# Seven-product pairs in the down projection, with one of their weight sums made ahead through HBM

## The chip, the cores and the metric

One Trainium2 chip, one of its NeuronCores. The metric is device time in microseconds (us) of one execution of the whole program; the kernel before takes 1456.75 us (median of 3 runs, 1456.52 to 1457.44). Everything is computed to fp32 quality: each factor x is split into a high part (`fp32r`, made by a copy on ScalarE) and a low part x - high (made by a subtraction on VectorE), and a product is the sum of high·high, high·low and low·high. One product of weights and activations is therefore three matmuls.

## The reference

One encoder layer over 256 tokens with a model width of 2048. What matters here is its second half:

```python
hf = rms_norm(x, ffn_norm)
g  = dwconv_centred(hf @ w_ffn_gate, conv_w, conv_b)       # 2048 -> 5632
x  = x + (gelu(g) * (hf @ w_ffn_up)) @ w_ffn_down          # 5632 -> 2048
gate_p = sigmoid(rms_norm(x, ple_norm) @ w_ple_gate)       # 2048 -> 2048
x  = x + gate_p * (p @ w_ple_proj)
out = rms_norm(x, final_norm)
```

Before it come one input projection, two attention branches, their projections, gates and an output projection.

## The kernel before, in words

The weights lie in HBM as a list of pieces of 128 x 2048 fp32 (1 MB), in the order of use. SyncE (SP) loads them one after another into three rotating buffers `raw` (L245). A piece is cut into units. For each unit ScalarE copies it to a high part `uh` or `vh` (L265) and VectorE subtracts to get the low part `ul` or `vl` (L266). Units made straight from the weights go through a ring of six, the `u` ring; units made from sums of weights go through a ring of two, the `v` ring. `drop` frees a unit when the last matmul on it is written, and `pump` then lets the next be made. TensorE (PE) consumes them.

The stages after the attention, in order, with the names used below:

- **E0 and E1**: the MLP halves. Each makes 22 chunks of 128 gate columns and 22 of up columns. One chunk of either is a *job*: 16 matmuls of 512 columns (L309) and 16 of 256 (L316), on one piece of weights. When a job is done `mlp` gathers it from PSUM (L447, L451); for every second gate chunk it does the convolution and gelu (L977 to L988), for every second up chunk the product (L997, L998), and it then splits the result into high and low (L1006, L1007, or L458, L459).
- **F00, F01 and F10, F11**: the down projection of the first and second half, each in two column ranges of 1024 of the model. One piece holds two chunks of rows (a *pair*) times two column blocks of 512, so it is a 2x2 by 2x2 block product. Kind `s` does it in eight products of 3 matmuls of 512 columns, 24 matmuls. Kind `S` does it in seven products, 21 matmuls, by sums of weights and sums of activations (a Strassen scheme). The sums of weights are made on VectorE from the loaded piece (L258 to L260), those of the activations by `sums_of` (L838 to L844).
- **pp0, pp1 and G0, G2, G3**: the per-layer embedding, its projection and the last gate. G0 also alternates seven and eight products; G2 and G3 do not.

`DOWN = "SsSsSsSsSss"` gives the kinds of the eleven pairs of each F stage: five of eleven by seven products. `ALT`, used by G0 among others, is `"SsSsSsSs"`. At the end of each F stage `row_sums` combines the seven products' accumulators on VectorE (L814 to L817) and adds them to the residual rows (L927, L929), while the last piece is still being multiplied.

Each engine runs its own instructions strictly in order, and that order is fixed when the program is built: a scheduler takes the program's order and its own estimate of costs, and may move instructions past one another unless they are marked with `keep`, which holds them in program order. `run_due` runs work that was put with `at` at a certain step of a stage: `at((stage, k), f)` runs `f` when the stage's loop reaches step k.

Of the kernel before, what the change touches and what calls it, by code (L numbers as in the profile page):

```python
# [16 lines left out]
P = 128  # L17
# [78 lines left out]
DOWN = "SsSsSsSsSss"  # L96
# [14 lines left out]
def _pieces():  # L111
# [8 lines left out]
    def quads(stage, n0, n1, pattern, k0=0):  # L120
        stages[stage] = range(len(pieces), len(pieces) + len(pattern))
        for i, c in enumerate(pattern):
            a, b = k0 + 2 * i, k0 + 2 * i + 1
            pieces.append((c, [(n0, a), (n1, a), (n1, b), (n0, b)]))
# [16 lines left out]
    for half in range(2):  # L141
        names = {"g": "w_ffn_gate", "u": "w_ffn_up"}
        jobs = [(names[kind], f) for kind, f in _ffn(half)]
        joint = 0 if half else JOINT
        e = [(name, k, f) for k in range(KC) for name, f in jobs[:joint]]
        e += [(name, k, f) for name, f in jobs[joint:] for k in range(KC)]
        blocks("E%d" % half, e)
        for s in range(2):
            quads("F%d%d" % (half, s), ("w_ffn_down", 2 * s * WIDE), ("w_ffn_down", (2 * s + 1) * WIDE),
                  DOWN, half * FHALF)  # L150
# [4 lines left out]
    quads("G0", ("w_ple_gate", 0), ("w_ple_gate", WIDE), ALT)  # L155
# [9 lines left out]
def _unit_list():  # L165

    units, of = [], []
    for p, (kind, _) in enumerate(_PIECES):
        if p == 0:
            cuts = [("n", a * P, b * P) for a, b in ((0, 1), (1, 4), (4, 7), (7, 11), (11, PIECE))]  # L170
        elif kind == "S":
            cuts = [("n", 0, WIDE), ("n", 2 * WIDE, 4 * WIDE), ("T13", 0, 2 * WIDE), ("T24", 2 * WIDE, 4 * WIDE)]
        else:
            cuts = [("n", 0, 2 * WIDE), ("n", 2 * WIDE, 4 * WIDE)]
        of.append(list(range(len(units), len(units) + len(cuts))))
        units += [(p, *cut) for cut in cuts]
    return units, of
# [11 lines left out]
def _encoder(ctx: ExitStack, tc, xt, pt, xrow, cols, gainrow, table, onehot, mask, ident_in, wts, out):  # L189
# [22 lines left out]

    flat = big.tile([P, KC + KC * T], F32, name="x", tag="R1")
# [28 lines left out]
    def load(r, a=0, b=PIECE):  # L242
        if a == 0:
            raws[r] = wpool.tile([P, PIECE * P], F32, name="raw", bufs=3)
        nc.sync.dma_start(raws[r][:, a * P:b * P], wts[r][:, a * P:b * P])  # L245
        state["raw"] = r + 1

    def produce():
# [7 lines left out]
        if kind == "T13":  # L256
            q = [raw[:, i * WIDE:(i + 1) * WIDE] for i in range(4)]
            nc.vector.tensor_tensor(raw[:, :2 * WIDE], raw[:, WIDE:3 * WIDE], raw[:, :2 * WIDE], op=ALU.subtract)  # L258
            nc.vector.tensor_tensor(q[2], q[2], q[0], op=ALU.subtract)
            nc.vector.tensor_tensor(q[3], q[3], q[2], op=ALU.subtract)  # L260
        src = raw[:, a:b]
# [4 lines left out]
        nc.vector.tensor_tensor(lo, src, hi.bitcast(F32), op=ALU.subtract)  # L266
        made[u] = (hi, lo)
# [105 lines left out]
    def quad_stage(stage, moving, combos=None, tags=("M2", "M3", "M4", "P22")):  # L373
# [24 lines left out]
        for i, p in enumerate(pieces):  # L398
            kind = _PIECES[p][0]
            us = _UNITS_OF[p]  # L400
            a, b = moving(2 * i), moving(2 * i + 1)
# [8 lines left out]
            else:  # L410
                s = combos(i)
                sums = [(s[:, 0, e], s[:, 1, e]) for e in range(4)]
                for g, (name, stationary, u, c, gone) in enumerate((
                        ("M1", part(a, 0), 0, 0, 0), ("M7", sums[2], 2, 1, None), ("M5", sums[0], 2, 0, 2),
                        ("M6", sums[1], 3, 0, None), ("M4", part(b, 1), 3, 1, 3),
                        ("M2", part(b, 0), 1, 1, None), ("M3", sums[3], 1, 0, 1))):
# [79 lines left out]
    def rms(i, total, key, columns=HALVES):  # L496
# [5 lines left out]
        at(i[0], ask)  # L502

# [103 lines left out]

    def view(a, offset, *dims):
        return bass.AP(tensor=a.tensor, offset=a.offset + offset, ap=[a.ap[0], *([step, n] for step, n in dims)])
# [223 lines left out]
    def sums_of(u, tag):  # L833
# [8 lines left out]
        s = tok.tile([P, 2, 4, P], FR, name="S", tag="S%d" % tag)  # L842
# [4 lines left out]
    combos = {}  # L847
# [113 lines left out]
    def activation_row(k):  # L961
        k %= FHALF
        return held["act"][1][k - 16] if 16 <= k < 20 else held["act"][k // 20 * 2][:, k - k // 20 * 20, :]
# [4 lines left out]
    def mlp(kind, n, acc):  # L968
# [21 lines left out]
        else:  # L990
# [8 lines left out]
            m = n % FHALF - 1  # L999
            if 16 <= m < 20:  # L1000
                for i in range(2):
                    halves(activation_row(m + i), u[:, i])
            else:
                i = m // 20 * 2
                d = held["act"][i][:, m - 10 * i:m - 10 * i + 2]
                nc.scalar.activation(d[:, :, :T], u, AF.Copy)  # L1006
                nc.vector.tensor_tensor(d[:, :, T:], u, d[:, :, :T].bitcast(F32), op=ALU.subtract)  # L1007
            pair = m // 2
            if DOWN[pair] == "S":
                combos["act", pair] = sums_of(u, pair // 2)  # L1010
# [13 lines left out]

    for half in range(2):
        held["act"] = [big.tile([P, 16, 2 * T], FR, name="act", tag="R1"),
                       [big.tile([P, 2 * T], FR, name="act1", tag="yb%d" % i) for i in range(4)],
                       held["tok"].tile([P, 2, 2 * T], FR, name="act2")]
# [159 lines left out]
```

## Time and profile before

| | |
|---|---|
| median of 3 runs | 1456.75 us (1456.52 to 1457.44) |
| the profiled execution's own time | 1457.09 us |
| its span, from the first to the last instruction | 1455.3 us, granted TensorE clock 0.998 |
| PE / VectorE / ScalarE busy | 1444.2 / 1196.8 / 838.7 us |
| HBM read, written | 279.49 MB, 2.14 MB |
| E0, F0 (F00 and F01), E1, F1 (F10 and F11) | 627 to 874, 874 to 987, 987 to 1232, 1232 to 1347 us of the span |
| pp0 and pp1, G0 to G3 | 1347 to 1360, 1360 to 1445 us |

The page counts a matmul as busy from its start to its modelled end, and consecutive matmuls overlap. So how fast PE really goes is read from the distance between the starts of two matmuls in the timeline, and a stall is a distance above the usual one. The same holds for VectorE: a 1024-wide operation is listed with 1.22 us, and the next one starts 1.14 us after it.

### The profile page before, as it was taken

To read this page: it belongs to the slowest core of one execution; us is meant where nothing else is said; L and a number is where in the kernel's file an instruction comes from. 1 tells how busy PE (TensorE), PEld (TensorE's weight loads), DVE (VectorE), ACT (ScalarE), POOL (GpSimd) and SP (SyncE) were. 2 spreads that over 40 slices of the span, in tenths; PEclk is the share of its full clock that TensorE was granted. 3 is DMA by queue.
4 is the path that set the end of the run, shared out by engine and by line. 5 is a ranking of instruction groups with operands and counts; after the bars stand their busy time and mean duration, and the time that the engine had idled before them with its cause. 6 is when DMAs were issued, how large, how long until landed. Compare 5 with 4: busy or idle time off the path is not lost.

```text
span 1455.3 us, 19303 instructions
## 1 busy us (share of the span) xinstructions
PE 1444.2 (99%) x7476; PEld 1234.3 (85%) x7476; DVE 1196.8 (82%) x1626; ACT 838.7 (58%) x1132; POOL 4.8 (0%) x9
## 2 busy tenths in 40 slices
PE   9999999999999999999999999999999999999997
PEld 8888888888888888888888888888888888888785
DVE  7677664679998989988787789987877778999994
ACT  7455544456555656666565565455655656565763
POOL 0000000000000000000000000000000000000000
PEclk9999999999999999999999999999999999999999
DMA  9653445535546456465555545465555554546462
GB/s 336 250 205 145 160 162 178 170 141 203 197 186 236 184 209 231 174 233 201 177 194 184 198 147 225 175 253 187 198 178 199 176 201 173 190 193 235 170 234 85
DMA packets 46455, 282.87 MB, mean 194 GB/s; under 512 B 4948, under 2 KB 9940, under 8 KB 14108
## 3 DMA queue, kind: packets, MB, share of 16 engines
q1 hardware_dynamic: 45644, 280.46, 52.8%
q8 instruction: 58, 0.95, 0.3%
q10 hardware_dynamic: 720, 1.19, 0.2%
q14 instruction: 33, 0.27, 0.1%
HBM read 279.49 MB, written 2.14 MB: 194 GB/s over the span
## 4 chain that ended last, share of the span: by engine, by line
PE 97%; DVE 1%; ACT 1%; issue 0%; DMA 0%; POOL 0%; POOLq 0%; DVEq 0%; SPq 0%; ACTq 0%
PE bank L309 29%; PE bank L316 15%; PE bank L366 14%; PE bank L367 14%; PE bank L368 14%; PE bank L355 2%; PE bank L357 2%; PE bank L293 2%; PE bank L356 2%; PE bank L294 1%; PE bank L861 1%; PE bank L678 0%; PE bank L626 0%; PE bank L625 0%; PE bank L624 0%
## 5 line engine op out<-in xcount | busy, mean ns | idle before, releaser
L265 ACT ACTIVATE uh<-raw 128x1024 fp32r<-128x1024 f32 (+2 forms) x519 | 523.1, 1015 | 394.0 <-PE bank L309 163.8
L266 DVE TENSOR_TENSOR ul<-raw,uh 128x1024 fp32r<-128x1024 f32 (+2 forms) x519 | 594.9, 1166 | 162.6 <-issue 81.0
L309 PE MATMUL bank<-hf,uh 128*128 128x512 f32 x1408 | 336.3, 391 | 0.0
L309 PEld LDWEIGHTS bank<-hf,uh 128*128 128x128 f32 x1408 | 258.9, 188 | 50.1
L316 PEld LDWEIGHTS bank<-hf,ul 128*128 128x128 f32 x1408 | 180.4, 191 | 6.7
L316 PE MATMUL bank<-hf,ul 128*128 128x256 f32 x1408 | 182.8, 283 | 0.0
L265 ACT ACTIVATE vh<-raw 128x1024 fp32r<-128x1024 f32 x92 | 97.0, 1056 | 42.4 <-DVE raw L258 22.9
L266 DVE TENSOR_TENSOR vl<-raw,vh 128x1024 fp32r<-128x1024 f32 x92 | 111.8, 1218 | 0.3
L309 PE MATMUL bank<-hs,uh 128*128 128x512 f32 x432 | 103.6, 392 | 0.0
L447 ACT ACTIVATE t<-bank 128x256 f32<-128x256 f32 x122 | 46.5, 383 | 97.4 <-PE bank L316 86.5
L309 PEld LDWEIGHTS bank<-hs,uh 128*128 128x128 f32 x432 | 79.5, 188 | 15.6
L366 PE MATMUL bank<-uh,act 128*128 128x512 f32 x232 | 90.4, 390 | 0.0
L367 PE MATMUL bank<-ul,act 128*128 128x512 f32 x232 | 90.4, 390 | 0.0
L368 PE MATMUL bank<-uh,act 128*128 128x512 f32 x232 | 90.2, 390 | 0.0
L366 PE MATMUL bank<-uh,hs 128*128 128x512 f32 x172 | 67.3, 391 | 0.0
L368 PE MATMUL bank<-uh,hs 128*128 128x512 f32 x172 | 67.2, 391 | 0.0
L367 PE MATMUL bank<-ul,hs 128*128 128x512 f32 x172 | 67.0, 389 | 0.0
L316 PE MATMUL bank<-hs,ul 128*128 128x256 f32 x432 | 56.6, 284 | 0.0
L258 DVE TENSOR_TENSOR raw<-raw 128x1024 f32<-128x1024 f32 x46 | 56.1, 1220 | 0.5
L316 PEld LDWEIGHTS bank<-hs,ul 128*128 128x128 f32 x432 | 54.5, 191 | 1.0
L367 PE MATMUL bank<-vl,S 128*128 128x512 f32 x138 | 54.0, 392 | 0.1
L366 PE MATMUL bank<-vh,S 128*128 128x512 f32 x138 | 54.1, 398 | 0.0
(242 smaller groups left out, 2229.4 us busy)
## 6 DMA issues: line engine op xcount, KB each, us to landing
raw<-in_wts SPq DMA_DIRECT2D x251, 1024.0 KB, 4.8
raw<-in_wts SPq DMA_DIRECT2D x12, 512.0 KB, 6.7
xr<-in_xrow SPq DMA_DIRECT2D x4, 512.0 KB, 8.2
x<-in_xt SPq DMA_DIRECT2D x13, 128.0 KB, 5.6
hb<-hold SPq DMA_DIRECT2D x3, 514.0 KB, 7.0
hb<-hold SPq DMA_DIRECT2D x2, 768.0 KB, 6.5
last<-in_gainrow SPq DMA_DIRECT2D x1, 1024.0 KB, 8.3
out<-xr SPq DMA_DIRECT2D x4, 256.0 KB, 2.6
```

Source lines behind the costliest of these rows:

```text
L258: nc.vector.tensor_tensor(raw[:, :2 * WIDE], raw[:, WIDE:3 * WIDE], raw[:, :2 * WIDE], op=ALU.subtract)
L265: nc.scalar.activation(hi, src, AF.Copy)
L266: nc.vector.tensor_tensor(lo, src, hi.bitcast(F32), op=ALU.subtract)
L293: nc.tensor.matmul(acc, hi[:, w], m, start=first, stop=False, skip_group_check=True)
L309: nc.tensor.matmul(acc, weights(u)[0][:, o * P:(o + 1) * P], m, start=first, stop=False, skip_group_check=True)
L316: nc.tensor.matmul(acc[:, T:], weights(u)[1][:, o * P:(o + 1) * P], m[:, :T], start=False, stop=last, skip_group_check=True)
L355: nc.tensor.matmul(acc[:, :n * P], xh, hi, start=(k == 0), stop=False)
L356: nc.tensor.matmul(acc[:, :n * P], xh, lo, start=False, stop=False)
L366: nc.tensor.matmul(acc, sh, wh, start=first, stop=False)
L367: nc.tensor.matmul(acc, sh, wl, start=False, stop=False)
L368: nc.tensor.matmul(acc, sl, wh, start=False, stop=last)
L447: keep(nc.scalar.activation(t, acc[:, T:], AF.Copy, scale=scale))
```

## The change

A third kind of piece, `Z`, takes the place of `S` in the F stages and in G0. It is a seven-product piece as well, 21 matmuls, with other sums: one sum of three of the four weight blocks is no longer made when the piece is used. It is made ahead, in the MLP halves: the three blocks are loaded once more (half the columns at a time, 128 x 3 x 256), VectorE makes the sum in two operations of 256 columns (L271, L272 of the new kernel), and ScalarE's queue stores it to a tile `ahead` in HBM (L275). When the piece is used, SP loads three of its blocks from the weights (L254) and the fourth place from `ahead` (L255). VectorE then makes the rest in one operation of 512 columns and one of 1024 (L282, L283), where `S` took one of 1024 and two of 512.

The first half's pattern becomes `ZZsZsZsZsZs`, six of eleven; the second half's keeps five of eleven. F00 and F01 each have one more seven-product piece, and each begins with two of them in a row. There are 12 `Z` pieces in F00 and F01, 10 in F10 and F11 and 4 in G0, so 24 half sums are made in E0 and 28 in E1. A half sum is asked for at step 9 of a job, added at step 8 of the next job, and stored at the beginning of the one after that, each held in program order. The activations of a `Z` pair are kept as the three blocks that the products use (`ends`) and the four sums (`S`), in other places than before (`places`, not shown).

```diff
-DOWN = "SsSsSsSsSss"
+DOWN = ("ZZsZsZsZsZs", "ZsZsZsZsZss")
+LASTS = 30
+ASK, ADD, STORE = 9, 8, None
...
+        elif kind == "Z":
+            cuts = [("n", WIDE, 2 * WIDE), ("n", 2 * WIDE, 4 * WIDE), ("T21", 0, 2 * WIDE), ("T03", 2 * WIDE, 4 * WIDE)]
...
+        if _PIECES[r][0] == "Z":
+            nc.sync.dma_start(raws[r][:, WIDE:], wts[r][:, WIDE:])
+            nc.sync.dma_start(raws[r][:, :WIDE], ahead.pop(r))
+        else:
+            nc.sync.dma_start(raws[r][:, a * P:b * P], wts[r][:, a * P:b * P])
...
+    def sum_ahead(p, h, tag):
+        cols = slice(h * T, (h + 1) * T)
+        if h == 0:
+            ahead[p] = dram.tile([P, WIDE], F32, name="ahead%d" % p)
+        q = held["tok"].tile([P, 3, T], F32, name="ahead", tag=tag) if isinstance(tag, str) else tag
+        keep(nc.sync.dma_start(q, wts[p][:, :3 * WIDE].rearrange("p (q c) -> p q c", c=WIDE)[:, :, cols]))
+        def add():
+            keep(nc.vector.tensor_tensor(q[:, 0], q[:, 2], q[:, 0], op=ALU.subtract))
+            keep(nc.vector.tensor_tensor(q[:, 0], q[:, 0], q[:, 1], op=ALU.add))
+        def store():
+            keep(nc.scalar.dma_start(ahead[p][:, cols], q[:, 0]))
+        return add, store
+    def sums_of_weights(raw):
+        q = [raw[:, i * WIDE:(i + 1) * WIDE] for i in range(4)]
+        nc.vector.tensor_tensor(q[1], q[0], q[1], op=ALU.subtract)
+        nc.vector.tensor_tensor(raw[:, 2 * WIDE:], raw[:, 2 * WIDE:], view(q[0], 0, (0, 2), (1, WIDE)), op=ALU.subtract)
...
+        behind = _PIECES[p][0] == "Z" == _PIECES[p - 1][0]
+        if kind == "T21" and not behind:
+            sums_of_weights(raw)
...
+        if behind and u == _UNITS_OF[p][1]:
+            sums_of_weights(raw)
...
+                else:
+                    todo = (("M1", m1, 0, 0, 0), ("M7", sums[2], 2, 1, None), ("M6", sums[1], 2, 0, 2),
+                            ("M5", sums[0], 3, 0, None), ("M4", m4, 3, 1, 3),
+                            ("M2", m2, 1, 1, None), ("M3", sums[3], 1, 0, 1))
...
+    def finish_ahead(stage):
+        for e in list(line):
+            e[0] += 1
+            if e[0] == 1:
+                at((stage, ADD), e[1])
...
+            elif e[0] == 2:
+                e[2]()
+                line.remove(e)
...
-        for kind, n in jobs[joint:]:
+        todo = [(p, h) for p in sevens(half) for h in range(2)]
+        for i, (kind, n) in enumerate(jobs[joint:]):
+            if i > 1 and todo and (i % 2 == 0 or i < LASTS):
+                held["job"] = todo.pop(0), ("act2", "S4")[i % 2]
+                one_ahead(stage)
+            finish_ahead(stage)
             mlp(kind, n, product(stage, lambda k: hf[:, k, :], KC, "e"))
+        assert not todo
+        drain_ahead()
```

How the built program differs is shown at two places of VectorE's order. The first is the middle of E0. Before, a job of the up kind has its gather (L451), the product (L997, L998) and two low parts (L266) there:

```order
L986 SCALAR_TENSOR_TENSOR gw<-gw 128x512
L451 TENSOR_TENSOR pair<-bank,t 128x256
L997 SCALAR_TENSOR_TENSOR pair<-pair,rms 128x512
L988 SCALAR_TENSOR_TENSOR gw<-gw 128x512
L998 TENSOR_TENSOR pair<-pair,gw 128x512
L266 TENSOR_TENSOR ul<-raw,uh 128x1024
```

With the change (lines of the new kernel: L500 is the gather, L306 the low part, L1111 the low part of activations, L271 and L272 the sum ahead) such a stretch of E0 is:

```order
L306 TENSOR_TENSOR ul<-raw,uh 128x1024
L1111 TENSOR_TENSOR act<-pair,act 128x2x256
L500 TENSOR_TENSOR gw<-bank,t 128x256
L271 TENSOR_TENSOR ahead<-ahead 128x256
L272 TENSOR_TENSOR ahead<-ahead 128x256
L306 TENSOR_TENSOR ul<-raw,uh 128x1024 x2
L500 TENSOR_TENSOR pair<-bank,t 128x256
L271 TENSOR_TENSOR ahead<-ahead 128x256
```

The two additions stand ahead of the next job's low parts, and whatever they wait for, the low parts wait for too. The second place is the end of F00 and the beginning of F01, where `row_sums` meets the first pieces of F01. Before:

```order
L266 TENSOR_TENSOR ul<-raw,uh 128x1024 x2
L266 TENSOR_TENSOR vl<-raw,vh 128x1024
L927 TENSOR_TENSOR xr<-xr,bank 128x512 x3
L929 TENSOR_TENSOR xr<-xr,c 128x1024
L266 TENSOR_TENSOR ul<-raw,uh 128x512
L266 TENSOR_TENSOR ul<-raw,uh 128x1024
L927 TENSOR_TENSOR xr<-xr,bank 128x512
```

With the change (L891 to L894, L1005 and L1007 are the row sums, L282 and L283 the sums of weights):

```order
L306 TENSOR_TENSOR vl<-raw,vh 128x1024
L282 TENSOR_TENSOR raw<-raw 128x512
L306 TENSOR_TENSOR vl<-raw,vh 128x1024
L306 TENSOR_TENSOR ul<-raw,uh 128x1024
L891 TENSOR_TENSOR c<-bank,c 128x512
L283 TENSOR_TENSOR raw<-raw 128x1024
L892 TENSOR_TENSOR c<-bank,c 128x512
L1005 TENSOR_TENSOR xr<-xr,bank 128x512
L893 TENSOR_TENSOR c<-bank,c 128x512
L894 TENSOR_TENSOR c<-bank,c 128x512
L1005 TENSOR_TENSOR xr<-xr,bank 128x512 x2
L1007 TENSOR_TENSOR xr<-xr,c 128x1024
```

After these come, in order, a fourth L1005, a `vl`, the other L1007 and a second `vl`: the low parts of the sums for the second seven-product piece of F01 stand behind the row sums of F00.

More of the change, by code (lines that the diff above doesn't have):

```diff
@@ L400, in quad_stage @@
             us = _UNITS_OF[p]
-            a, b = moving(2 * i), moving(2 * i + 1)
+            if (stage, i) not in ends:
+                a, b = moving(2 * i), moving(2 * i + 1)
             if kind == "s":
@@ L502, in rms, with one_ahead, ask, drain_ahead @@
         at(i[0], ask)
+    line = []
+    def one_ahead(stage):
+        job, where = held["job"]
+        def ask():
+            line.append([0, *sum_ahead(*job, where)])
+        at((stage, ASK), ask)
+    def finish_ahead(stage):
[3 more added lines that the diff above has]
+                at((stage, ADD), e[1])
+                if STORE is not None:
+                    at((stage, STORE), e[2])
+                    line.remove(e)
+            elif e[0] == 2:
+                e[2]()
+                line.remove(e)
+    def drain_ahead():
+        for e in line:
+            if e[0] == 0:
+                e[1]()
+            e[2]()
+        del line[:]
     due, rt, rc, held = {}, {}, {}, {}
```

94 lines of the change are left out of this document (65 added, 29 removed).

## The prediction

> **What bounds the kernel now.** First the page: busy times and the shares of the chain of waits that ended last.
>
> ```profile
> span 1455.3 us, 19303 instructions
> PE 1444.2 (99%) x7476; PEld 1234.3 (85%) x7476; DVE 1196.8 (82%) x1626; ACT 838.7 (58%) x1132; POOL 4.8 (0%) x9
> PE 97%; DVE 1%; ACT 1%; issue 0%; DMA 0%; POOL 0%; POOLq 0%; DVEq 0%; SPq 0%; ACTq 0%
> ```
>
> PE is 97% of the chain. A busy PE need not be at its pace, so I looked for its pace in the timeline, in F00:
>
> ```profile
> 885.36 0.39 PE L366 MATMUL bank<-vh,S 128*128 128x512 f32 x1
> 885.58 0.39 PE L367 MATMUL bank<-vl,S 128*128 128x512 f32 x1
> 885.81 0.39 PE L368 MATMUL bank<-vh,S 128*128 128x512 f32 x1
> ```
>
> A matmul is listed with 0.39 us, but the next starts 0.227 us after it. The windows by stage (PE, PEld, DVE, ACT, POOL busy) say that this is the pace of whole stages:
>
> ```profile
> 627.00:875.00 248.00, 248.00 (x1431) 219.20 (x1430) 195.84 (x289) 149.56 (x210) 0.71 (x1) 1.00 0.53 189
> 875.00:987.00 112.00, 112.00 (x495) 92.58 (x494) 102.79 (x111) 59.30 (x64) 0.00 (x0) 1.00 0.56 211
> 987.00:1232.00 245.00, 245.00 (x1409) 216.50 (x1408) 188.88 (x273) 144.59 (x196) 0.00 (x0) 1.00 0.52 186
> 1232.00:1347.00 115.00, 115.00 (x515) 94.87 (x514) 110.26 (x132) 66.38 (x79) 0.00 (x0) 1.00 0.57 211
> ```
>
> In F0 (second row) 495 matmuls take 112 us, 0.2263 us each: there is no stall to speak of. VectorE, however, is busy 102.8 of these 112 us (92%), and 110.3 of 115 in F1. So PE sets the end, and VectorE is the engine that could take its place. How near it is shows in the timeline after the row sums of F00, VectorE first and then PE:
>
> ```profile
> 941.82 1.22 DVE L266 TENSOR_TENSOR vl<-raw,vh 128x1024 fp32r<-128x1024 f32 x1
> ...
> 943.16 0.39 PE L366 MATMUL bank<-vh,S 128*128 128x512 f32 x1
> 943.38 0.39 PE L367 MATMUL bank<-vl,S 128*128 128x512 f32 x1
> ```
>
> The low part is ready at 941.82 + 1.22 = 943.04 us and used at 943.38: 0.34 us of cover at the tightest place. In E the cover is long. A low part is made when PE frees a place in the ring of six units, half a job each, and it is used about two and a half jobs later; a job is 16 x (0.227 + 0.120) = 5.55 us, so the cover is some 14 us.
>
> **What the change removes.** F00 and F01 each turn one piece of 24 matmuls into one of 21; the order of PE is the same up to the end of E0 and has 6 matmuls fewer in all. 6 x 0.227 = **1.36 us**, all of it on the path. That is the whole gain in work: five of eleven stays in F1, and G0 has as many seven-product pieces as before.
>
> A page of the Trainium skill sets the price of a matmul otherwise: TensorE: Matmul & The Clock Gate, section Back-to-back issue gap, gives about 131 ns sustained at 512 columns, and 216 ns for an isolated gap. By these the six would be worth 0.79 or 1.29 us. The trace disagrees with the first, and I keep 0.227.
>
> **VectorE in F and G.** The prices, as distances between starts:
>
> ```profile
> 847.65 0.28 DVE L838 TENSOR_TENSOR cmb<-pair 128x128 f32<-128x128 f32 x1
> 847.85 0.28 DVE L839 TENSOR_TENSOR cmb<-pair 128x128 f32<-128x128 f32 x1
> ...
> 866.69 0.68 DVE L259 TENSOR_TENSOR raw<-raw 128x512 f32<-128x512 f32 x1
> 867.29 0.68 DVE L988 SCALAR_TENSOR_TENSOR gw<-gw 128x512 f32<-128x512 f32 x1
> 867.89 0.68 DVE L260 TENSOR_TENSOR raw<-raw 128x512 f32<-128x512 f32 x1
> 868.49 1.22 DVE L266 TENSOR_TENSOR vl<-raw,vh 128x1024 fp32r<-128x1024 f32 x1
> 869.63 0.68 DVE L997 SCALAR_TENSOR_TENSOR pair<-pair,rms 128x512 f32<-128x512 f32 x1
> ...
> 876.98 0.42 DVE L451 TENSOR_TENSOR pair<-bank,t 128x256 f32<-128x256 f32 x1
> 877.31 1.22 DVE L258 TENSOR_TENSOR raw<-raw 128x1024 f32<-128x1024 f32 x1
> ```
>
> 128 columns 0.20, 512 columns 0.60, 1024 columns 1.14, 256 columns 0.33 us. Low parts cost an `s` piece 2 x 1.14 = 2.28 us, an `S` piece 0.60 + 3 x 1.14 and its sums 1.14 + 2 x 0.60, together 6.36; a `Z` piece saves one 512-wide operation, 5.76. PE needs 24 x 0.227 = 5.45 and 21 x 0.227 = 4.77. F0 had 10 x 6.36 + 12 x 2.28 = 91.0 us of this on VectorE and gets 12 x 5.76 + 10 x 2.28 = 91.9: as much work in 1.36 us less. F1 is relieved by 10 x 0.60 = 6.0 us, which buys nothing where PE does not wait. G0 is relieved by 2.4, and there PE does wait once:
>
> ```profile
> 1373.58 0.39 PE L367 MATMUL bank<-ul,pl 128*128 128x512 f32 x1
> 1374.05 0.50 PE L367 MATMUL bank<-vl,S 128*128 128x512 f32 x1
> 1374.39 0.39 PE L368 MATMUL bank<-vh,S 128*128 128x512 f32 x1
> ```
>
> 0.47 and 0.34 instead of 0.227: 0.36 us lost to a late `vl`. Two `Z` pieces ahead of it save 1.2 us on VectorE. I take **0.3 us** gained (0 to 0.36).
>
> What is new in F0 is where the work falls: F00 and F01 begin with two seven-product pieces, 11.52 us of VectorE against 9.54 of PE. *At the start of F00* the last free moment of VectorE is this one, and PE starts F00 at the second row:
>
> ```profile
> 862.86 0.69 DVE L266 TENSOR_TENSOR ul<-raw,uh 128x512 fp32r<-128x512 f32 x1
> ...
> 874.34 0.40 PE L366 MATMUL bank<-vh,S 128*128 128x512 f32 x1
> ```
>
> From that low part on, VectorE's order holds, down to the second piece's last `vl`, 9 operations of 1024, 11 of 512, 4 of 256 and 5 of 128 columns: 10.3 + 6.6 + 1.3 + 1.0 = 19.2 us, so they end at 882.1 us. PE uses that `vl` as its 36th matmul of the stage, at 874.34 + 35 x 0.227 = 882.3. So it is just in time if VectorE waits for nothing. I take 0.3 us of stall (0 to 2.0, which is 11.52 less 9.54).
>
> *At the start of F01* the sums' ring of two decides where VectorE can begin. F00's pieces are then 21 or 24 matmuls each, 246 in all: F00 ends at 874.34 + 246 x 0.227 = 930.2, its tenth piece begins 45 matmuls earlier, at 920.0, and its first sums unit is free after 9 matmuls, at 922.0. F01's first `vl` cannot end before 922.0 + 1.06 (the high part on ScalarE) + 1.22 = 924.3. From it to the second piece's last `vl` stand four low parts and a sum of 1024, a sum of 512, and for the row sums eight of 512 and two of 1024: 7 x 1.14 + 9 x 0.60 = 13.4 us, 937.7. PE needs it 10 matmuls into the second piece, at 930.2 + 31 x 0.227 = 937.2. I take **0.6 us** of stall. Its bounds: below, 0; above, all that the demand exceeds PE from the tenth piece on, (3 x 5.76 + 2.28 + 7.08 for the row sums) - (3 x 4.77 + 5.45) = 6.9 us, if the cover in the rings counts for nothing.
>
> **The sums ahead in E.** Each costs VectorE 2 x 0.33 us: 24 x 0.66 = 15.8 us in E0 and 28 x 0.66 = 18.5 in E1. E0 has 248 - 196 = 52 idle us and E1 56. They lie in the middle jobs, and the last 14 jobs have none, so the crowded end of E0 is left alone. ScalarE issues 52 stores, 0.45 us each by the two rows of the end, on an engine that is 60% busy in E:
>
> ```profile
> 1444.82 0.90 ACTq L1132 DMA_DIRECT2D out<-xr  x2
> ```
>
> The new loads, 384 KB each, go through SP's queue among the weights. Nothing of their kind is in the trace; the nearest rows (KB, median us from issue to landing) are:
>
> ```profile
> raw<-in_wts SPq DMA_DIRECT2D x251, 1024.0 KB, 4.8
> xr<-in_xrow SPq DMA_DIRECT2D x4, 512.0 KB, 8.2
> pair<-in_pt SPq DMA_DIRECT2D x1, 256.0 KB, 6.7
> ```
>
> Issued behind a piece of weights, 256 KB took 6.7 and 512 KB 8.2 us; I take 7.5. Where an addition waits for such a load, the next job's low parts wait behind it, and behind them the loads of the next weights. The load ahead of it on SP waits for the low part of an earlier piece. Between that low part and the addition stand, by the rows of the order at the prices above, 4.2 us of VectorE's work in the tightest case (the stretch of E0 that is shown) and 6 to 12 in most. With 7.5 us E0's 24 additions wait some 27 us in all if VectorE never idles, against 52 - 15.8 = 36 us of idle time and 14 us of cover. So VectorE runs later and PE sees nothing: **0 us**.
>
> **The weights of a `Z` piece** come in two loads instead of one, 768 and 256 KB. Over F0 the high parts (ScalarE's copies; the last figures are idle time and who ended it) wait little for weights:
>
> ```profile
> L265 ACT ACTIVATE uh<-raw 128x1024 fp32r<-128x1024 f32 x35 | 36.4, 1056 | 29.3 <-PE bank L368 21.2 <-DMA raw<-in_wts 7.7
> ```
>
> 7.7 us in all, on units that are used about 10 us after they are made. A second issue and a landing that is a microsecond later use some of that, and I put it at nothing; without that cover it would add to the stall at F01.
>
> **The sum**, against the profiled execution's 1457.09 us: - 1.36 - 0.3 + 0.3 + 0.6 = 1456.33. The median is 0.34 us below that execution, which makes 1455.99: **1456.0 us**.
>
> **The rivals.** What a measurement of this kernel can tell from no change is about 0.2%, 2.9 us.
>
> *No stall at all*: VectorE finds the work at both heads in time, G0's wait goes: 1456.75 - 1.36 - 0.36 = 1455.0. It is for this that the two margins above are a few tenths. Same side, 0.19. To be faster by 0.2%, more must go: the small PE waits of F1 and pp, around the transposes,
>
> ```profile
> 1348.64 0.39 PE L368 MATMUL bank<-uh,u 128*128 128x512 f32 x1
> 1349.02 0.66 PE L861 MATMUL bank<-ident,xr 128*128 128x128 f32 x4
> ```
>
> such as this of 0.15 us, are about 1.2 us together; with all of them 1453.8, exactly at the bound. They go with transposes and not with a late VectorE, so 0.05.
>
> *VectorE becomes the bound at the heads of F00 and F01.* Price: up to 2.0 + 6.9 = 8.9 us, so 1456.75 - 1.36 + 8.9 = 1464.3. For it: 92% busy, 0.34 us of cover, and a scheduler's order in which a `vl` stands behind four row sums that wait for PE. Against it: the sums row by row above, which miss by tenths. It makes the kernel slower from 2.9 + 1.36 = 4.3 us of stall on. 0.09.
>
> *The additions hold up VectorE in E.* If a load takes 10 us, the additions of E0 wait some 64 us against 36 + 14, and PE runs 14 us late in each half: 1456.75 - 1.4 + 28 = 1483. It decides from about 9 us of landing. Against it: 8.2 us for a larger load. 0.05. A rule of the Trainium skill stands on its side, in DMA: Bandwidth & Descriptors, section Issuing engines are not separate DMA queues: transfers started by different engines run on the same 16 DMA engines and interleave, so the stores on ScalarE's queue are not free for the weights. In this trace those engines are 53% busy in E.
>
> That the change does not do what it says is left out: the built order has the six matmuls fewer and the 52 pairs of additions.
>
> **The numbers.** Forecast 0.62, no stall 0.19: together 0.81 within 0.2%. Faster 0.05, slower 0.09 + 0.05 = 0.14. The range goes from 1454.3, below the rival without stalls, to 1459.3, which takes in 3.3 us more stall than I expect.
>
> **What would show it.** Right: F0 shorter by about a microsecond with distances above 0.227 only near its start and at 935 to 938 us; additions in E idle before them, waiting for DMA, and no stall of PE there. Wrong: stalls of PE in E with `ul` late, or a row of stalls through F0 with VectorE near 100%.

## The result and the profile after

| | before | the change |
|---|---|---|
| median | 1457.05 us (1456.52 to 1457.44, 4 runs) | 1475.49 us (1469.90 to 1476.37, 4 runs) |
| ratio, 95% interval | | 1.0117 [1.0105, 1.0129] |
| the profiled execution, its span | 1457.09, 1455.3 us | 1469.90, 1468.1 us |

By the ratio the change is slower by 1.2%, some 17 us, clear of the noise. The forecast was 1456.0 us, no change. The page of the change, in the rows that answer to those shown of before, and its groups and DMA issues of the new work:

```profile
span 1468.1 us, 19718 instructions
PE 1446.1 (99%) x7470; PEld 1234.3 (84%) x7470; DVE 1224.2 (83%) x1730; ACT 829.4 (56%) x1148; POOL 4.9 (0%) x9
HBM read 299.94 MB, written 8.95 MB: 210 GB/s over the span
PE 83%; DVE 7%; DMA 6%; issue 2%; ACT 1%; SPq 0%; POOLq 0%; POOL 0%; DVEq 0%; ACTq 0%
L271 DVE TENSOR_TENSOR ahead<-ahead 128x256 f32<-128x256 f32 x52 | 22.0, 423 | 62.2 <-DMA ahead<-in_wts 62.0
ahead<-in_wts SPq DMA_DIRECT2D x52, 384.0 KB, 4.0
ahead<-ahead ACTq DMA_DIRECT2D x52, 128.0 KB, 4.1
```

PE has the six matmuls fewer (7470 against 7476), yet its share of the chain of waits has gone from 97% to 83%, and VectorE and DMA hold 13% of it. The fifth row names the new wait: the first of the two additions of the sums ahead (L271) is kept waiting for its load for 62.0 us. The sixth says that a slow load is not the reason: it lands 4.0 us after its issue, where the prediction took 7.5.

The stages, from the start of a stage's first matmul to that of the next stage's, the last one to the start of the last matmul, in us (worked out from the timeline's starts; the second profile of the change is experiment 9, the four tiles are experiment 1):

| stage | before | change, first profile | change, second profile | four tiles |
|---|---|---|---|---|
| E0 | 247.10 | 250.64 | 255.14 | 247.10 |
| F0 | 113.02 | 114.32 | 114.21 | 112.19 |
| E1 | 244.90 | 253.95 | 255.02 | 244.91 |
| F1 | 114.52 | 114.40 | 114.39 | 114.37 |
| pp and G | 98.43 | 97.51 | 97.52 | 97.54 |
| span | 1455.3 | 1468.1 | 1473.6 | 1453.3 |

Of the 12.8 us of the first profile E0 and E1 have 12.6: the MLP halves, in which PE was to see nothing. The windows of the change (us, then busy time of PE, PEld, DVE, ACT, POOL with counts, clock, DMA share, GB/s) say where in them:

```profile
627.00:795.00 168.00, 168.00 (x968) 148.32 (x968) 137.34 (x230) 92.93 (x141) 0.71 (x1) 1.00 0.68 240
795.00:835.00 40.00, 37.74 (x213) 32.42 (x212) 30.59 (x49) 19.50 (x30) 0.00 (x0) 1.00 0.75 252
835.00:878.00 43.00, 43.00 (x251) 38.11 (x250) 41.06 (x61) 30.37 (x45) 0.00 (x0) 1.00 0.56 203
992.00:1127.00 135.00, 135.00 (x776) 119.23 (x775) 103.65 (x166) 68.45 (x97) 0.00 (x0) 1.00 0.70 243
1127.00:1190.00 63.00, 56.13 (x312) 47.51 (x311) 49.21 (x87) 31.02 (x48) 0.00 (x0) 1.00 0.70 238
1190.00:1246.00 56.00, 56.00 (x325) 49.54 (x324) 53.28 (x81) 37.40 (x57) 0.00 (x0) 1.00 0.59 221
```

In each half PE is busy without a break for 135 us or more, most of them with sums ahead being made; then it idles (the second and the fifth row), and after the last sum it idles no more. VectorE is not full in the stretches with stalls (30.6 of 40, 49.2 of 63), and 7.9 of the 9.4 us that it idles in the second row are waits for loads of sums (summed from the timeline). So it is no lack of VectorE's time, and it is something that builds up: a delay that grows job by job until the cover of some 14 us is gone.

### What delays the loads

SP's waits in the change (total us, times, longest), and below them the chain of waits over one stall of E1:

```profile
SPq L268 <- DMA ahead<-ahead: 168.2, 42, 8.1
```

```profile
1136.34 2.77 DMA ahead<-ahead
1139.11 0.02 issue
1139.13 6.28 DMA ahead<-in_wts
...
1145.50 0.17 DVE ahead L271
1145.67 4.38 DMA ahead<-in_wts
1150.05 0.02 issue
1150.07 0.04 DVE ahead L271
1150.10 0.31 issue
1150.41 1.22 DVE ul L306
```

and what PE did then, in the timeline:

```profile
1147.76 1.11 PE L358 MATMUL bank<-hf,ul 128*128 128x256 f32 x8
1151.68 1.22 PE L358 MATMUL bank<-hf,ul 128*128 128x256 f32 x8 [2.81 <-DVE ul L306]
```

Read the chain from the top. A store of a finished sum (`ahead<-ahead`, to HBM) lands at 1139.11. Only then does SP issue the load of a later sum, 0.02 us after it; the load lands 6.28 us later, the addition L271 starts at once; the next sum's load lands at 1150.05, its addition starts at once; the low part behind it (L306, 1150.41 + 1.22 = 1151.63) releases PE at 1151.68, 2.81 us late.

The reason is in two words of the diff: `("act2", "S4")[i % 2]`. The sums use two tiles in turn. A load into a tile has to wait until the store that still reads it has landed, the store of the sum two before. SP, which waits for it, does so 42 times, 168.2 us in all. Of the 29 sums for which the trace has both times within one half, 24 were asked for within 0.15 us of that store's landing. So there is a loop: load, landing, addition on VectorE, store in ScalarE's order, landing, and the next load into the same tile. One turn of it in the middle of E0, taken from the issues and landings of that tile:

| us | |
|---|---|
| 696.12 | SP issues the load of the fifth sum |
| 701.54 | it lands, VectorE adds from 701.63 |
| 702.55 | ScalarE issues the store |
| 707.85 | it lands |
| 707.93 | SP issues the load of the seventh sum |

One turn makes two sums, one in each tile. They are due in two jobs of PE, 11.1 us, and the turns take longer: from the fifth load (696.12) to the 23rd (809.87) there are nine, (809.87 - 696.12) / 9 = 12.6 us each, and ten in E1 of 12.9 us (1036.51 to 1165.80). The turns are uneven, from 8.0 to 18.2 us in E0: besides the two landings a turn has the addition's wait for its place in VectorE's order (1.6 us on average there, up to 6.6) and the store's wait for its place in ScalarE's (2.2 us, up to 10.2). Each sum thus comes some 0.8 us (E0) or 0.9 us (E1) later against PE than the one before it. VectorE's order puts the low parts behind the additions, so they too come that much later in each job, and 16 to 18 sums of it use up the 14 us of cover. The turns run at this pace from the fifth sum of E0 on, and the first stall above 0.2 us, at 806.7 us, is at the 22nd. This is why PE idles only late in each half. The trace shows the cover going. Two low parts of E0 on VectorE, an early and a late one, and below each the matmuls on PE that read it first:

```profile
684.49 1.22 DVE L306 TENSOR_TENSOR ul<-raw,uh 128x1024 fp32r<-128x1024 f32 x1
699.90 2.08 PE L358 MATMUL bank<-hf,ul 128*128 128x256 f32 x16
...
792.98 1.22 DVE L306 TENSOR_TENSOR ul<-raw,uh 128x1024 fp32r<-128x1024 f32 x1
794.54 2.28 PE L358 MATMUL bank<-hf,ul 128*128 128x256 f32 x16
```

The first is ready 14.2 us before its use (699.90 - 685.71), the second 0.34 us. In the kernel before, the same distance stays at 12.8 us or more from 690 us to the end of E0.

Another way to the same loss would be the weights themselves, whose loads stand behind those of the sums on SP. It is not what happens: in the chain of waits from 992 to 1246 us (E1) the loads of the sums hold 21%, their stores 11%, and the loads of weights nothing.

### The profile page after: what moved, and what is told of

It is laid out like the page before. It is cut to its first block, busy times and chain, and to the rows that moved or that the text cites. A ratio compares the mean times of both kernels' runs of the same rounds, so it can differ in the third digit from the quotient of the medians.

```text
span 1468.1 us, 19718 instructions
## 1 busy us (share of the span) xinstructions
PE 1446.1 (99%) x7470; PEld 1234.3 (84%) x7470; DVE 1224.2 (83%) x1730; ACT 829.4 (56%) x1148; POOL 4.9 (0%) x9
## 4 chain that ended last, share of the span: by engine, by line
PE 83%; DVE 7%; DMA 6%; issue 2%; ACT 1%; SPq 0%; POOLq 0%; POOL 0%; DVEq 0%; ACTq 0%
PE bank L351 19%; PE bank L408 14%; PE bank L409 14%; PE bank L410 14%; PE bank L358 10%; DMA ahead<-in_wts 4%; DVE ul L306 3%; DMA ahead<-ahead 2%; PE bank L397 2%; PE bank L399 2%; PE bank L398 2%; PE bank L335 2%; PE bank L336 1%; PE bank L939 1%; DVE gw L1085 1%
## 5 line engine op out<-in xcount | busy, mean ns | idle before, releaser
L306 DVE TENSOR_TENSOR ul<-raw,uh 128x1024 fp32r<-128x1024 f32 (+2 forms) x519 | 595.0, 1164 | 92.8 <-ACT uh L305 64.5
L358 PEld LDWEIGHTS bank<-hf,ul 128*128 128x128 f32 x1408 | 180.6, 191 | 17.3 <-DVE ul L306 10.6
L305 ACT ACTIVATE vh<-raw 128x1024 fp32r<-128x1024 f32 x96 | 101.2, 1058 | 58.4 <-DVE raw L282 26.7
L306 DVE TENSOR_TENSOR vl<-raw,vh 128x1024 fp32r<-128x1024 f32 x96 | 116.2, 1220 | 1.1
L410 PE MATMUL bank<-uh,act 128*128 128x512 f32 x218 | 84.9, 390 | 0.0
L409 PE MATMUL bank<-ul,act 128*128 128x512 f32 x218 | 84.8, 389 | 0.0
L408 PE MATMUL bank<-uh,act 128*128 128x512 f32 x218 | 84.6, 390 | 0.0
L271 DVE TENSOR_TENSOR ahead<-ahead 128x256 f32<-128x256 f32 x52 | 22.0, 423 | 62.2 <-DMA ahead<-in_wts 62.0
L409 PEld LDWEIGHTS bank<-ul,act 128*128 128x128 f32 x218 | 40.9, 188 | 8.6
L410 PEld LDWEIGHTS bank<-uh,act 128*128 128x128 f32 x218 | 40.9, 188 | 8.5
```

Of the source, the lines that this page charges most:

```text
L305: nc.scalar.activation(hi, src, AF.Copy)
L358: nc.tensor.matmul(acc[:, T:], weights(u)[1][:, o * P:(o + 1) * P], m[:, :T], start=False, stop=last, skip_group_check=True)
L408: nc.tensor.matmul(acc, sh, wh, start=first, stop=False)
L409: nc.tensor.matmul(acc, sh, wl, start=False, stop=False)
L410: nc.tensor.matmul(acc, sl, wh, start=False, stop=last)
```

## The experiments

Each kernel below is the changed kernel with the edit shown. In those with an edit in the sums' tiles the line numbers behind it are three higher: the load is then L271 instead of L268, the additions L274 and L275 instead of L271 and L272. The kernel before took 1457.12 us (25 runs) beside experiments 1 to 4, 1457.04 (31 runs) beside 5 to 8, 1457.04 (7 runs) beside 9.

### 1. Four tiles instead of two

```diff
-                held["job"] = todo.pop(0), ("act2", "S4")[i % 2]
+                held["job"] = todo.pop(0), ("act2", "vh", "S4", "vl")[i % 4]
...
+        if tag in ("vh", "vl"):
+            q = held["tok"].tile([P, 4 * T], F32, name="ahead", tag=tag, bufs=2)[:, :3 * T].rearrange("p (q c) -> p q c", c=T)
```

The two other names are those of the `v` ring, which the middle of the MLP halves doesn't use. Each of them has two places (`bufs=2`), so the four names are six places; "four tiles" stands for this below.

> The change, but the sums ahead rotate over the two tiles and both rings of the v units (which stand empty in the middle of E) instead of over two tiles alone, so a load no longer waits for the store of two sums before. Loop theory (an addition, its store, the landing of the store, the next load into that tile and its landing form a loop that is longer than two jobs): SP no longer waits for stores (168 us with two tiles), E0 and E1 return to 247 to 248 and 245 to 246 us of PE, F00's stall of 2.3 us falls below 1 us, time 1455 to 1459 us. Work theory (35 us more of VectorE's additions and 27 MB more of transfers are too much for E whatever the tiles): E0 and E1 stay at 250 and 252 us or more, time 1468 to 1477 us.

Measured: 1454.85 us (1454.29 to 1455.54), ratio 0.9985 [0.9975, 0.9994]. Its wait rows of SP and its DMA issues:

```profile
SPq L271 <- DMA ahead<-ahead: 4.3, 8, 2.0
```

```profile
ahead<-in_wts SPq DMA_DIRECT2D x52, 384.0 KB, 6.2
ahead<-ahead ACTq DMA_DIRECT2D x52, 128.0 KB, 4.7
```

SP's waits for stores are gone (4.3 us instead of 168.2), and VectorE waits for no load of a sum. The loads take longer than in the change, 6.2 instead of 4.0 us (why, no run shows), and it doesn't matter. E0 and E1 are back at 247.10 and 244.91 us, with the same sums, loads and stores made. So neither the work on VectorE nor the 20 MB more from HBM costs PE anything; the two tiles did. It also has the lowest median of the kernels here, 2.3 us (0.15%) below the kernel before; experiments 3, 5 and 6 are within 0.02% of it by the ratio, which is less than the noise.

### 2. The store earlier

```diff
-ASK, ADD, STORE = 9, 8, None
+ASK, ADD, STORE = 9, 8, 12
```

The store is put at step 12 of the job in which the sum is added, instead of the start of the next: four of sixteen steps, 1.4 us, shorter a loop.

> The change with two tiles, but a store is put at step 12 of the job of its addition instead of at the beginning of the next job. Loop theory: the loop is shorter by up to one job on ScalarE's queue, SP waits for stores less than half of 168 us, time 1457 to 1466 us. Work theory: 1468 to 1477 us, as the change.

Measured: 1465.74 us (1464.63 to 1472.49), 1.0068 [1.0045, 1.0091]. By the ratio about 10 us of the 17 remain:

```profile
SPq L268 <- DMA ahead<-ahead: 201.6, 38, 9.4
DVE ahead L271 <- DMA ahead<-in_wts: 52.7, 17, 4.9
```

E1 takes 250.41 us, 3.5 less than in the change, and F0 112.13, 2.2 less, without a stall at its head; E0 takes 250.93, no less. The median falls in the range expected, but SP's waits were expected to fall below half of 168 us and rose to 201.6. So it is not the length of that wait that costs: SP may wait long, as long as the load comes before the addition needs it. VectorE's waits for loads fell from 62.0 to 52.7 us, in 17 waits instead of 30.

### 3. No stores

```diff
             elif e[0] == 2:
-                e[2]()
                 line.remove(e)
...
-            nc.sync.dma_start(raws[r][:, :WIDE], ahead.pop(r))
+            nc.sync.dma_start(raws[r][:, :WIDE], wts[r][:, :WIDE])
...
```

The sums are loaded and added as before but not stored, and the fourth place of a `Z` piece is loaded from the weights, so the products use another sum than they should. Two tiles, as in the change.

> The change without the 52 stores: the sums are loaded and added in E as before, but not stored, and a Z piece takes its first block straight from the weights (so its products are those of other sums; the number of operations and bytes in F and G is the same). Loop theory: nothing waits for a store, E0 and E1 return to 247 to 248 and 245 to 246 us, time 1455 to 1459 us. If the loads or the additions are what E cannot carry: 1468 to 1477 us.

Measured: 1455.00 us (1453.80 to 1455.71), 0.9985 [0.9976, 0.9995]; E0 247.10, E1 244.91 us.

```profile
SPq L268 <- DVE ahead L272: 44.8, 31, 3.1
DVE ahead L271 <- DMA ahead<-in_wts: 20.7, 11, 2.2
```

A load into a tile now waits only for the additions that read it. Two tiles are enough without the stores, and VectorE may wait 20.7 us for loads without a loss for PE. This leaves the store, its place in ScalarE's order and its landing, as the part of the loop that makes it too long. Experiment 2 shows that the place counts; what the landing is worth by itself no run shows, since none changes it alone.

### 4. Six of eleven, sums made in place

```diff
-DOWN = ("ZZsZsZsZsZs", "ZsZsZsZsZss")
+DOWN = ("SSsSsSsSsSs", "SsSsSsSsSss")
...
-    quads("G0", ("w_ple_gate", 0), ("w_ple_gate", WIDE), ALT.replace("S", "Z"))
+    quads("G0", ("w_ple_gate", 0), ("w_ple_gate", WIDE), ALT)
...
```

No sums ahead at all; the sixth pair of F00 and F01 has its sums made when it is used, as the kernel before does for five.

> Six of eleven by seven products in the first half, as in the change and with its places for the activations, but with all sums of weights made where the piece is used (kind S): no sums ahead, no loads and stores of them. E0 and E1 are as in the kernel before, 247 and 245 us, by every theory. F0: 1.36 us less of matmuls, and 12 x 0.60 us more of VectorE than with Z. If VectorE at the heads of F00 and F01 is the bound (the third rival of the prediction), stalls of 3 to 8 us, 1459 to 1464 us; if the cover holds, 0.5 to 2 us of stalls, 1456 to 1458 us.

Measured: 1457.36 us (1456.72 to 1458.11), 1.0002 [0.9992, 1.0011]: no change. F0 takes 113.25 us against 113.02 before, though it has the six matmuls fewer. The largest stall, PE in the timeline, and the high part on ScalarE (ACT) that it waits for:

```profile
939.83 0.39 PE L410 MATMUL bank<-vh,S 128*128 128x512 f32 x1
940.77 0.50 PE L408 MATMUL bank<-vh,S 128*128 128x512 f32 x1 [0.56 <-ACT vh L305]
939.66 1.06 ACT L305 ACTIVATE vh<-raw 128x1024 fp32r<-128x1024 f32 x1 [2.05 <-DVE raw L297]
```

0.94 us between two starts instead of 0.227, at the head of F01. The high part had waited for the last of the sums made in place (L297) on VectorE. The stalls of F0 together cost 1.6 us more than before (113.25 - 113.02 + 1.36), and the six matmuls are 1.36 us. So the sixth pair gains nothing while its sums are made in place, for which VectorE lacks the time, at the head of F01 above all.

### 5 and 6. Three tiles, and three tiles with a longer loop

The tile `vh` is made as in experiment 1.

```diff
-                held["job"] = todo.pop(0), ("act2", "S4")[i % 2]
+                held["job"] = todo.pop(0), ("act2", "vh", "S4")[i % 3]
```

So `act2` and `S4` come round every third sum. `vh` has two places and comes round every sixth, which makes four places in all.

Experiment 6 does besides this the addition and the store one job later, which makes the way from a load to its store a job longer:

```diff
-            if e[0] == 1:
+            if e[0] == 2:
                 at((stage, ADD), e[1])
...
-            elif e[0] == 2:
+            elif e[0] == 3:
...
```

> Four tiles' run with a third of the sums in each of the two tiles and a third in one ring of the v units, so a tile of the two is used again by the third sum after it. In the change's profile two sums take 12.6 us in E0 (from the load at 696.1 to that at 809.9 us, 9 pairs) and 12.9 us in E1, where two jobs of PE take 11.1. Loop theory: three jobs take 16.65 us, more than the 12.6 to 12.9 of the loop, so no stall in E: E0 247, E1 245 us, 1454 to 1456 us, the same as with four tiles. If it is only the number of sums in flight that counts, three would lie between two and four: 1457 to 1466 us.

> Three tiles as in the run beside it, but addition and store come one job later after the load. Loop theory: the loop grows by a job, to 18.2 to 18.5 us, against the 16.65 us of three jobs; each sum is then 0.5 to 0.6 us late, 12 to 17 us over 24 to 28 sums, about the cover in the ring: SP waits for stores again, 40 us or more, and E0 and E1 are 0 to 4 us longer each, 1454 to 1463 us. If the wait of VectorE for a load that has not landed were the cause by itself, the later addition would help: VectorE's wait for loads near 0 and no wait of SP for stores, 1454 to 1456 us.

Measured: 1455.33 us (1454.98 to 1456.35), 0.9987 [0.9978, 0.9997], and 1455.04 us (1454.71 to 1455.81), 0.9986 [0.9977, 0.9995]. E0 and E1 are 247.10 and 244.90 us in both. The waits of SP and of VectorE, first of experiment 5, then of 6:

```profile
SPq L271 <- DMA ahead<-ahead: 108.3, 25, 8.3
DVE ahead L274 <- DMA ahead<-in_wts: 19.5, 13, 3.5
```

```profile
SPq L271 <- DMA ahead<-ahead: 109.6, 28, 7.7
DVE ahead L274 <- DMA ahead<-in_wts: 21.3, 13, 3.6
```

One name more is enough for PE to lose nothing: a turn of `act2` or `S4` may now take three jobs, 3 x 5.55 = 16.7 us, where with two tiles it had two. SP still waits for stores for 108 us: what counts is whether a turn fits into the jobs that it spans, not that someone waits in it.

It fits only just. The turns are not the 12.6 us of two tiles: from a load to the third load after it are 17.1 us in E0 and 16.8 in E1 on average (from the fifth sum on), with the longer way of experiment 6 17.3 and 16.7. So the cover still shrinks. The shortest distance from a finished low part to its use, after the first sums, is 9.4 us in E0 and 8.7 in E1 in experiment 5, and 6.6 and 10.1 in experiment 6, against 12.0 with four tiles and 0.05 in the change. It comes back when the sums end. Whether it would last for a longer row of sums is not shown.

Experiment 6 was expected to make E0 and E1 0 to 4 us longer if a job's delay were simply added to the turn, 12.6 + 5.55 = 18.2 us. They are not longer, and the turns take what they take in experiment 5. So a turn is not a fixed sum of its parts. There are waits in it, for a load or for a place in an engine's order, and that they shrank by what the delay added is likely but not shown. The rival, that SP would not wait for stores at all, fell as well (109.6 us).

### 7. Six of eleven in both halves, with four tiles

```diff
-DOWN = ("ZZsZsZsZsZs", "ZsZsZsZsZss")
+DOWN = ("ZZsZsZsZsZs", "ZZsZsZsZsZs")
```

> Four tiles, and six of eleven by seven products in the second half too: 6 matmuls less in F10 and F11, 1.36 us, and 4 more half sums in E1. If VectorE's cover in F1 holds as it does in F0 with four tiles: 1453 to 1454.5 us. If F1, where VectorE has more to do (the next stage's turns and sums), has stalls of 1 us or more: 1454.5 to 1458 us.

Measured: 1455.82 us (1454.82 to 1456.66), 0.9991 [0.9981, 1.0], no better than with five in the second half. The six matmuls fewer of F1 come back as stalls, the largest at the head of F11, where its first seven-product piece asks for a bank of PSUM that the row sums of F10 on VectorE (L895) have not read yet:

```profile
1287.98 0.39 PE L413 MATMUL bank<-uh,ends 128*128 128x512 f32 x1
1289.25 0.47 PE L411 MATMUL bank<-vh,S 128*128 128x512 f32 x1 [0.88 <-DVE c L895]
```

1.27 us between two starts; all stalls of F1 are 1.76 us, against 0.44 in the kernel before. G0 has one of 0.53 us besides, for a late `vl`.

### 8. Five of eleven in both halves, with four tiles

```diff
-DOWN = ("ZZsZsZsZsZs", "ZsZsZsZsZss")
+DOWN = ("ZsZsZsZsZss", "ZsZsZsZsZss")
```

> Four tiles, but five of eleven in both halves as before: kind Z and its sums ahead alone, without the sixth pair. By the account of the profiles (the sixth pairs are worth 1.36 us less 0.5 us of stalls in F0; pp and G gain 0.9 us from Z) the time is 0.8 to 0.9 us above that with six: 1455.2 to 1456.7 us. If the sums ahead in E cost anything that the four tiles do not hide, it is at or above the kernel before, 1457 us.

Measured: 1456.28 us (1455.47 to 1456.64), 0.9994 [0.9985, 1.0003]. F0 takes 113.03 us, as before, and pp and G 97.55. By the ratios the sums ahead alone are worth 0.06%, 0.8 us, and the sixth pair another 0.09%, 1.3 us; either is within the intervals, which are 0.09% to each side. The stages of the profiles say 0.9 us for the first (pp and G, 98.43 to 97.55) and 0.8 us for the second (F0, 113.03 to 112.19).

### 9. The change once more

Nothing is edited. The first profile was that of the quickest of four executions, so what the others lost was in no trace.

> The changed kernel itself once more, nothing edited: its profiled execution took 1469.9 us, its other three some 1475.5, and the 5.6 us between are in no trace yet. If the loop of the two tiles sets it, an execution of 1475 us has them in E0 and E1 (together 18 us longer than before, where the first profile has 12.6), with SP's waits for stores above 168.2 us, and F and G as in the first profile within 1 us. Rival: the rest comes from the down projection's heads; then E0 and E1 stay at 250.6 and 254.0 us and F0 or F1 grows by 5.

Measured: 1474.29 us (1470.22 to 1475.35), 1.0110 [1.0093, 1.0127]; the profiled execution 1475.35 us, span 1473.6. E0 is 8.0 us longer than before and E1 10.1, together 18.2 us of the 18.3 by which the span is longer; F and G are those of the first profile within 0.11 us. The waits of SP and of VectorE in this execution:

```profile
SPq L268 <- DMA ahead<-ahead: 171.8, 42, 7.8
DVE ahead L271 <- DMA ahead<-in_wts: 65.0, 31, 4.3
```

So the whole loss lies in the two stages with the two tiles, as the loop's theory expected. The first stall of E0 above 0.2 us is at 777.8 us here, at 806.7 in the first profile: the loop runs a little slower, and the cover is gone some five jobs earlier. Why the loop is slower in the one execution than in the other is not settled; in E0, which has 4.5 of the 5.5 us between the two spans, the granted clock is 1.00 in both.

## Why the prediction was wrong

**The step that failed** is the term of the sums ahead in E, "So VectorE runs later and PE sees nothing: **0 us**". It measured 12.6 us in the first profile and 18.2 in the second. Its premise was a queue: "The load ahead of it on SP waits for the low part of an earlier piece", as if the loads of the sums could go out whenever SP came to them. The prediction had the order of SP but not what the load itself waits for. The tile's earlier use, two sums before, with the landing of its store at the end, stood in the diff (two names and `i % 2`) and was not followed; in 52 loads SP waited for it 42 times.

One number of that step came out right, by luck. It expected E0's additions to wait "some 27 us in all", and those of the first profile wait 27.7 us, in 14 waits (summed from the timeline). But the 27 came from landings of 7.5 us, and the loads land after 4.0; they are late because they are issued late. And it set the 27 us against a fund of 36 us of idle time and 14 of cover, and not all of the idle time was to be had. In the stretch from 795 to 835 us, where PE stalls, VectorE idles 9.4 of 40 us, and 7.9 of these are the waits themselves. The cover of 14 us was right in size, as the trace shows. But the delay adds up, which a sum of waits over a stage doesn't show: 0.8 us per sum against 14 us of cover is a yes or no by the number of sums, some 17, where E0 has 24 and E1 28.

**The rival on that side**, "*The additions hold up VectorE in E*", had the place and the sign, with a chance of 0.05, and 1483 us for it; and what the prediction named as a sign of being wrong, stalls of PE in E with a late `ul`, is what the trace shows. Its condition was wrong: it was to decide from about 9 us of landing, and the loads land after 4.0 us. The landing that matters is that of the store (4.1 us, at times 6.9, as from 751.91 to 758.79 us), and with it the store's place in ScalarE's order; the prediction priced the store only as an issue on ScalarE. The rule of the Trainium skill that stood beside it, DMA: Bandwidth & Descriptors, section Issuing engines are not separate DMA queues, was not what decided: in experiment 1 the same loads and stores keep the 16 engines busy for 0.68 and 0.70 of E0 and E1 (0.53 and 0.52 before), and PE loses nothing. Whether the shared engines lengthen the stores' landing no run shows.

```profile
627.00:874.00 247.00, 247.00 (x1426) 218.31 (x1425) 211.08 (x342) 148.35 (x215) 0.71 (x1) 1.00 0.68 241
987.00:1231.00 244.00, 244.00 (x1404) 215.65 (x1403) 206.74 (x332) 142.52 (x201) 0.00 (x0) 1.00 0.70 246
```

These windows of experiment 1 also show what E would have been by the prediction: VectorE 15 to 18 us busier, PE busy in every microsecond.

**The six matmuls, -1.36 us**: right. F0 of experiment 1 is 112.19 us, 0.83 below before, with some 0.5 us of stalls that before has not, together 1.3 to 1.4.

**The head of F00, +0.3 us for a late `vl`**: in the change it is 2.27 us, and of another cause. PE in the timeline, and VectorE:

```profile
879.99 0.39 PE L408 MATMUL bank<-uh,ends 128*128 128x512 f32 x1
882.49 0.47 PE L408 MATMUL bank<-uh,ends 128*128 128x512 f32 x1 [2.11 <-DVE pair L500]
```

```profile
880.59 1.21 DVE L283 TENSOR_TENSOR raw<-raw 128x1024 f32<-128x1024 f32 x1
881.73 0.28 DVE L918 TENSOR_TENSOR cmb<-pair,cmb 128x128 f32<-128x128 f32 x1
881.93 0.74 DVE L500 TENSOR_TENSOR pair<-bank,t 128x256 f32<-128x256 f32 x2
```

PE waits for a bank whose gather of the last job of E0 (L500) stands behind the sums of the next piece on VectorE. With four tiles the distances at this head are 0.21 us too long in all (experiment 1). In the change the gather starts 4.0 us after F00's first matmul, in experiments 1 and 2, which have no such stall, 1.9 us. It is thus what is left of E0's lateness. With four tiles the term of 0.3 is right in size, but by luck: what is left stands at these same two matmuls, and no stall at a late `vl` is seen.

**The head of F01, +0.6 us**: 0.28 us in the change and in experiment 1, within its bounds of 0 to 6.9; the term was twice too large.

**G0, -0.3 us**: the direction was right, but pp and G together gained 0.9 us (98.43 to 97.51). The stalls there fell from 1.31 to 0.44 us. The prediction counted only the one wait that it had found, and left the others, "about 1.2 us together", to a rival, since they go with transposes; in pp and G about half of them went after all, in F1 nearly none (0.44 to 0.36 us).

**The weights of a `Z` piece in two loads, 0**: right; no stall of F above 0.2 us waits for them.

Without the failed step, and with the other terms as measured, the sum is - 1.36 - 0.9 + 0.2 + 0.3 = -1.8 us. The profile of experiment 1 is 2.0 us shorter than that of before, and its median 2.3 us lower, inside the range that was stated.

## What to carry to other kernels

When a diff loads into a buffer, follow that buffer round its whole loop, from the load to the moment at which it may be loaded again; if its last reader is a store, the loop ends with the store's landing. Compare the turn with the time that the consumer leaves until the same buffer is wanted again: 12.6 us do not fit into two jobs of 5.55 us. With three jobs nothing was lost, but the turn had grown to 17 us, so leave more room than the sum says. A loop that misses by less than a microsecond is invisible while the cover lasts, so look at the end of a stage, and don't set waits of one moment against an engine's idle time of another.

## What the runs showed of the hardware

The small stores to HBM are not quick here: 128 KB land after 4.1 us (median, the change) to 4.7 us (experiment 1). In the change that is as long as a load of 384 KB takes (4.0 us). The Trainium skill, in DMA: Bandwidth & Descriptors, section Anatomy of one DMA — SWDGE (gpsimd) path, gives for another way of issuing a fixed cost of about 2.0 us, most of it the receipt of the last write, heaviest for HBM, and a rate by which 128 KB would add 0.3 us, an estimate of 2.3 us. The time here is nearly twice as long, on engines that are about 0.7 busy in E; how much of it is the receipt no run shows.

A stall of PE can cost more than its own length. In the second profile of the change, the windows around one of the two stalls of E1:

```profile
1150.00:1155.00 5.00, 3.08 (x21) 2.59 (x20) 3.73 (x7) 1.06 (x1) 0.00 (x0) 1.00 0.87 313
1155.00:1159.00 4.00, 4.00 (x13) 3.22 (x13) 3.33 (x6) 3.26 (x5) 0.00 (x0) 0.57 0.92 309
1159.00:1163.00 4.00, 4.00 (x26) 3.61 (x26) 3.97 (x7) 2.81 (x6) 0.00 (x0) 1.00 0.72 232
```

After a stall of about 2 us the granted clock is 0.57 over 4 us (0.50 from 1155.1 to 1158.5 us, 3.4 us), and 13 matmuls are done in them instead of 26; the distances between 512-wide matmuls are 0.427 us there instead of 0.227. It happens again from 1186 to 1193 us, and once in the profile of experiment 2 (0.50 from 1171.0 to 1174.4 us), each time within 1.2 us of the end of a stall of 2.0 us. In the first profile a stall of 2.81 us, shown above, had no such stretch behind it. The Trainium skill, in TensorE: Matmul & The Clock Gate, section What's actually happening, says that the clock is halved after at least one idle window of about 3.4 us, which runs freely. The halving agrees with the 0.427 us; the stalls here, of about 2 us, are shorter than that window, and what decides whether the clock falls these runs don't tell. In E1 of that execution it accounts for up to 4.5 us (8 matmuls of 0.2 us and then 9 of 0.09 and 10 of 0.2), not all of it lost, since low parts that come late would have stopped PE in any case: E1 is only 1.1 us longer than in the first profile.
